# Column order of the split products in a hybrid decoder step: four interleaved sets of runs of 4 in place of two sets or one run

## The chip, the cores and the metric

The kernel runs on one core of a Trainium2 chip. The metric is the device time of one execution in microseconds, the median over repeated runs. A profiled execution, taken by the hardware profiler, gives the trace. TensorE does the matrix products, VectorE (DVE), ScalarE (ACT) and GpSimd (POOL) the element work, SyncE (SP) and others issue transfers. SBUF holds the operands, PSUM the results of TensorE, in banks of 512 fp32 columns on 128 partitions.

## The reference

One step of a one-layer decoder over 512 prompt rows and 64 sample rows (8 sequences of 8), everything in fp32, width 2048. The large products are the ones that matter here:

```python
h = rms_norm(x, g_mix) @ w_in            # 2048 -> 5128: q, k, v, forget gates, conv inputs
attn = fox_attention(q, k, v, logf)      # prompt: causal; sample: paged cache of 2048 rows
cy = conv_heads(u_ext, ...)              # gated, causal depthwise convolution, layer norm
x = x + concatenate([rms_norm(attn), cy]) @ w_out          # 2048 -> 2048
hid = square(relu(rms_norm(x, g_mlp) @ w_up))              # 2048 -> 8192
x = x + hid @ w_down                                       # 8192 -> 2048
gate = sigmoid(rms_norm(x, g_ple) @ w_ple_gate)            # 2048 -> 2048
y = rms_norm(x + (pe @ w_ple) * gate, g_final)             # pe: 256 -> 2048
```

## The kernel before

All activations lie transposed, features on the 128 partitions and the 576 rows (512 prompt, 64 sample) as columns. A product's moving operand and its result are 288 columns (`HR`), half of the rows, and both halves together make the 576. The weights, 128 x 128 blocks, are the stationary operand.

**Split products.** For precision every fp32 operand is split in two parts of the type fp32r: the rounded value ("hi") and the rest ("lo"). A product is then three matmuls into the same PSUM columns: hi x hi, hi x lo, lo x hi. ScalarE makes the hi parts (`split_hi`, line 160, and line 134 for the streamed weights), VectorE the lo parts (`split_lo`, line 163, and line 140).

**First phase** (to about 990 us). `mm6` (line 526) is the one place of its split products: three pairs of hi and lo, and in each pair the two halves of the columns, `r` = 0 and 1, into the two banks of one result `U`. The moving operands are `xh` and `xl`, the normed input; the weights `whi` and `wlo` come through `WStream`. It makes the input projection, the output projection and the projection of the per-layer input (there with the operands `px`). Between its products run the attention and the convolution: the cache pages (`k`, `v`) are read by lines 890 and 929, line by line paced by a credit per product. The forget gates' small projection (line 570) has 16 weight columns, reads the same `xh` and `xl`, and has no reordered columns.

**Second phase** (from about 990 us). `phase2` walks a list of weight blocks in the order of `plan`. For the up projection (`g` = 1) and the down projection (`g` = 2), each a 2 x 2 block product is made of seven products instead of eight: sums of weight blocks on one side (VectorE, lines 1913 to 1915) and of operand halves on the other, listed in `PRODS`. Each of the seven writes a bank `P` of its own; lines 1687 to 1689 are the three matmuls of one product. Line 1807 and its neighbours (`combine_head`, `combine_tail`) put the seven results together. The gate projection (`g` = 3, 4, 5) is made by `plain`, lines 1758 to 1760, in the ordinary way: the first block of outputs with both halves of the columns (`g` = 3), then the seven others for the first half of the columns (`g` = 4), then the same seven for the second half (`g` = 5), so that the end of the kernel has half the columns to finish.

**Order of columns.** `braid` (lines 91 and 92) changes the order in which a matmul walks its 288 columns, without moving any data. It sees the columns as (b a c): `c` neighbours form a run, `a` runs in a row belong to `a` different sets. It then goes through all runs of set 0, then all of set 1, and so on. Operand and result are walked in the same order, so every column still lands at its own place. Before, `a` is always 2. Line 526 uses `c` = 24: six runs of 24, then the other six. Lines 1687 to 1689 use `c` = 8: 18 runs of 8, then the other 18. `plain` uses `c` = 8 where both halves are in work (`g` = 3) and no reordering, one run of 288, where only one is (`g` = 4 and 5).

The order of the instructions on every engine is written out by the program (a manual schedule), with a queue of side work (`Beside`) that is charged by estimated costs; these costs do not depend on the order of columns.

Of the kernel before, what the change touches and what calls it, by code (L numbers as in the profile page):

```python
# [20 lines left out]
HR = 288  # L21
# [66 lines left out]
    return ap.bitcast(F32)  # L88


def braid(t, c):
    return t.rearrange("p (b a c) -> p a b c", a=2, c=c)


class Shift:
# [10 lines left out]
def EL(n):  # L106

    return n / 960.0 + 0.07
# [45 lines left out]
class Kern:  # L154
# [367 lines left out]
    def mm6(self, u, wh, wl, xh, xl, first, last):  # L522

        for n, (w, x) in enumerate(((wh, xh), (wh, xl), (wl, xh))):
            for r in range(2):
                self.nc.tensor.matmul(braid(u[:, r, :HR], 24), w, braid(x[:, r * HR:(r + 1) * HR], 24),  # L526
                                      start=first and n == 0, stop=last and n == 2)

    def chunk(self, u, c, k0, k1):
# [897 lines left out]
    def phase2(self):  # L1427
        tc, nc, a = self.tc, self.nc, self.a
# [36 lines left out]
        def rows_of(g):  # L1465
            return {3: (0, 1), 4: (0,), 5: (1,)}[g]
# [188 lines left out]
        for t, (si, k) in enumerate(quadlist):  # L1655
            g, p, *_ = segs[si]
            ks = self.orders[si]
            n, i = len(ks), t - seg0[si]
            if prev:
                pg, ppr, c, r, pfinal, pp_ = prev  # L1660
                if pg >= 3:
                    cost = self.plain_end(ppr, c, rb)
                else:
                    cost = self.combine_tail(ppr, EL)
                    c = c[0]
                bg.spend(cost)
                late = (pg, pp_) == (1, 31)
                fin_of[pg, pp_] = bg.add(2 if late else 0, fins[pg](pp_, c, r, pg if pg >= 3 else pfinal))
                if not late:
                    recent.append(fin_of[pg, pp_])  # L1670
                prev = None
            s = slots[min(g, 3), k]
            if s.work is not None:
                bg.flush(s.work)
                s = slots[min(g, 3), k]
            bg.spend(W.prep(t + 2))
            hi, lo = W.hl.pop(t)
            if i == 0:
                pr = {}
            if g >= 3:  # L1680
                self.plain(pr, hi, lo, s, i == 0, i == n - 1, rows_of(g))
            else:
                for (q, ia, ib) in self.PRODS:
                    if i == 0:
                        pr[q] = self.P_()
                    o, xh, xl = braid(pr[q][:, :HR], 8), braid(s.hi[:, ib, :], 8), braid(s.lo[:, ib, :], 8)
                    nc.tensor.matmul(o, hi[:, ia, :], xl, start=(i == 0), stop=False)  # L1687
                    nc.tensor.matmul(o, hi[:, ia, :], xh, start=False, stop=False)  # L1688
                    nc.tensor.matmul(o, lo[:, ia, :], xh, start=False, stop=(i == n - 1))  # L1689
            for fn in hooks.get(t, ()):  # L1690
                fn()
            if g == 2 and p in (4, 5, 6) and i in (0, 2):
                bg.nudge(2)
            slow = p == 0 and g != 2
            if i == (n - 2 if g < 4 else 5) and not slow:
                if g > 1:
                    bg.flush_all(0)
                r = pre[g](p, lastseg[g, p] == si)
            dt = (2.79, 3.18, 1.59, 1.59)[max(g - 2, 0)]
            if i == n - 1:  # L1700
                bg.wait(1000 + t, dt)
            else:
                bg.run(1000 + t, dt)
            if g == 1 and p == 0 and i + 2 < n and slots[1, ks[i + 2]].work:
                bg.flush(slots[1, ks[i + 2]].work)
            if i == n - 1:
                if g > 1:
                    bg.flush_all(0)
                if slow:
                    r = pre[g](p, lastseg[g, p] == si)  # L1710
                if recent[0]:
                    bg.flush(recent[0])
                if g >= 3:
                    c = t2.tile([128, 2, NR], F32, name="c", tag="c", bufs=3)
                else:
                    c = self.combine_head(pr, cx if (g, p) == (1, 31) else None)
                    bg.spend(2 * EL(HR))
                prev = (g, pr, c, r, lastseg[g, p] == si, p)
# [3 lines left out]
        pg, ppr, c, r, pfinal, p = prev  # L1722
        c, acc = c[:, :, :HR], self.acc2[:, HR:]
# [16 lines left out]
        o = next(rs)[:, None, :HR].broadcast_to([128, 2, HR])  # L1740
# [5 lines left out]
    def plain(self, pr, hi, lo, s, first, last, halves):  # L1746

        nc = self.nc
        for nh, blocks in enumerate(((2, 3), (0, 1))):
            for kh, ia in enumerate(blocks):  # L1750
                for r in halves:
                    if first and kh == 0:
                        pr[nh, r] = self.P_()
                    rows = slice(r * HR, r * HR + HR)
                    o, xh, xl = pr[nh, r][:, :HR], s.hi[:, kh, rows], s.lo[:, kh, rows]
                    if len(halves) == 2:
                        o, xh, xl = braid(o, 8), braid(xh, 8), braid(xl, 8)
                    nc.tensor.matmul(o, hi[:, ia, :], xh, start=first and kh == 0, stop=False)  # L1758
                    nc.tensor.matmul(o, hi[:, ia, :], xl, start=False, stop=False)  # L1759
                    nc.tensor.matmul(o, lo[:, ia, :], xh, start=False, stop=last and kh == 1)  # L1760
# [287 lines left out]
```

## Time and profile before

| | |
|---|---|
| median of 3 runs (lowest to highest) | 2654.57 us (2654.18 to 2655.11) |
| profiled execution | 2659.14 us |
| its span, first to last instruction | 2657.4 us |
| mean granted TensorE clock | 0.997 of full |
| busy share: TensorE, its weight loads, VectorE, ScalarE, GpSimd | 98%, 96%, 77%, 44%, 20% |
| TensorE instructions | 21,910 matmuls, 21,910 weight loads |
| moved by DMA | 543.87 MB, mean 205 GB/s |

How to read it. The profile's page lists groups of instructions: line, engine, operation, result<-operands, partitions x elements, the count, the busy time in us, the mean ns of one, and behind the bar the idle time before them with what ended it. A matmul is pipelined: its row lasts longer than the distance to the next one's start, so the mean ns of one is not what it costs in a stream. The distance from start to start is. The trace gives it by the window view (for a stretch of time: its length, and for each engine the busy time and the number of instructions, then granted clock, DMA share and GB/s; the order of the engines is TensorE's matmuls, its weight loads, VectorE, ScalarE, GpSimd), by the timeline (start in us, length in us, engine, line, operation, count), and by the chain of work that ended last in order of time (start, length, engine, result, line, count). All columns of a matmul are shown as one number (128x288) whatever their order.

### The profile page before, as it was taken

Reading aid. Unit: us, or ns where it says so; the run is one execution under the profiler, and the core shown is the slowest. Engines: PE = TensorE matmul, PEld = TensorE weight load, DVE = VectorE, ACT = ScalarE, POOL = GpSimd, SP = SyncE. Lnnn points to the kernel's source line nnn. Section 1 sums busy time; section 2 is a strip of 40 time slices with the busy share of each in tenths; the row PEclk is TensorE's granted clock in tenths of the full one; section 3 lists DMA queues with packets and bytes.
Section 4 is the critical chain, followed back from the end, with each engine's and each line's share of the span. In section 5 each row is a group of like instructions: output and inputs, shape, how many; then the busy total and the mean of one; then the engine's idle time right before and its main releaser. Section 6 shows DMA issues by size and latency. Waiting matters only on the chain.

```text
span 2657.4 us, 56481 instructions
## 1 busy us (share of the span) xinstructions
PE 2615.8 (98%) x21910; PEld 2539.0 (96%) x21910; DVE 2040.2 (77%) x3552; ACT 1166.7 (44%) x1714; POOL 527.4 (20%) x942
## 2 busy tenths in 40 slices
PE   9999999999999999999999999999999999999997
PEld 8999999888999999999999999999999999999997
DVE  6577778656564459889988888898888888898676
ACT  5222233245453335445554444554444444444554
POOL 2288787611020000000000000110000000000110
PEclk9999999999999999999999999999999999999998
DMA  6698998999764564444544444776575565656675
GB/s 206 207 309 289 309 294 293 301 322 325 239 222 128 183 212 144 152 143 160 171 158 143 142 143 142 256 197 196 153 205 145 165 174 169 176 188 216 199 244 166
DMA packets 240367, 543.87 MB, mean 205 GB/s; under 512 B 26049, under 2 KB 27074, under 8 KB 240098
## 3 DMA queue, kind: packets, MB, share of 16 engines
q1 hardware_dynamic: 170402, 325.97, 38.3%
q0 software_dynamic: 36160, 153.32, 18.2%
q10 hardware_dynamic: 33536, 60.96, 7.1%
q8 instruction: 172, 2.82, 0.4%
q14 instruction: 97, 0.79, 0.1%
HBM read 445.33 MB, written 94.83 MB: 203 GB/s over the span
## 4 chain that ended last, share of the span: by engine, by line
PE 87%; DVE 6%; DMA 4%; issue 2%; ACT 1%; SPq 0%; POOL 0%; ACTq 0%; DVEq 0%; POOLq 0%
PE U L526 24%; PE P L1687 16%; PE P L1689 16%; PE P L1688 16%; PE P L1759 2%; PE P L1760 2%; PE P L1758 2%; PE D L890 2%; PE O L929 2%; DVE w2l L163 1%; DMA wraw<-in_w_main 1%; DMA w2r<-in_w_down 1%; DMA k<-in_cache_kv 1%; DMA xs<-dl 1%; PE S L784 1%
## 5 line engine op out<-in xcount | busy, mean ns | idle before, releaser
L1687 PE MATMUL P<-xs,w2h 128*128 128x288 f32 x3584 | 1060.2, 296 | 12.1 <-DVE c L1807 7.2
L1688 PE MATMUL P<-xs,w2h 128*128 128x288 f32 x3584 | 1052.1, 294 | 0.0
L1689 PE MATMUL P<-xs,w2l 128*128 128x288 f32 x3584 | 1050.0, 293 | 0.5 <-DVE w2l L163 0.5
L160 ACT ACTIVATE w2h<-w2r 128x896 fp32r<-128x896 f32 (+1 forms) x632 | 558.9, 890 | 755.4 <-PE P L1688 420.8
L163 DVE TENSOR_TENSOR w2l<-w2r,w2h 128x896 fp32r<-128x896 f32 (+1 forms) x632 | 637.7, 1011 | 192.6 <-ACT w2h L160 190.3
L1687 PEld LDWEIGHTS P<-xs,w2h 128*128 128x128 f32 x3584 | 674.0, 188 | 19.5 <-DVE c L1807 10.3
L1689 PEld LDWEIGHTS P<-xs,w2l 128*128 128x128 f32 x3584 | 675.2, 188 | 1.5 <-DVE w2l L163 1.4
L1688 PEld LDWEIGHTS P<-xs,w2h 128*128 128x128 f32 x3584 | 673.6, 188 | 0.2 <-issue 0.2
L526 PE MATMUL U<-xh,whi 128*128 128x288 f32 x1792 | 397.2, 303 | 0.2 <-ACT xh L160 0.2
L526 PE MATMUL U<-xl,whi 128*128 128x288 f32 x1792 | 380.5, 293 | 0.8 <-DVE xl L354 0.7
L526 PE MATMUL U<-xh,wlo 128*128 128x288 f32 x1792 | 379.9, 293 | 0.1
L526 PEld LDWEIGHTS U<-xh,whi 128*128 128x128 f32 x1792 | 283.3, 188 | 18.9 <-issue 16.7
L134 ACT ACTIVATE whi<-wraw 128x512 fp32r<-128x512 f32 x224 | 140.8, 629 | 353.2 <-PE U L526 298.6
L526 PEld LDWEIGHTS U<-xl,whi 128*128 128x128 f32 x1792 | 284.8, 188 | 1.9 <-DVE xl L354 1.9
L526 PEld LDWEIGHTS U<-xh,wlo 128*128 128x128 f32 x1792 | 284.8, 188 | 0.3 <-DVE wlo L140 0.3
L140 DVE TENSOR_TENSOR wlo<-wraw,whi 128x512 fp32r<-128x512 f32 x224 | 160.2, 716 | 111.7 <-ACT whi L134 111.2
L1078 DVE SCALAR_TENSOR_TENSOR y<-ue,cv,y 128x512 f32<-128x512 f32 x240 | 183.5, 765 | 5.3
L1913 DVE TENSOR_TENSOR w2r<-w2r 128x512 f32<-128x512 f32 (+1 forms) x273 | 177.7, 651 | 11.8 <-DMA w2r<-in_w_down 11.8
L1079 POOL TENSOR_SCALAR cvt<-us,cv 128x64 f32<-128x64 f32 x240 | 161.2, 672 | 22.3
L1760 PE MATMUL P<-xs,w2l 128*128 128x288 f32 x512 | 150.9, 295 | 1.1 <-DVE w2l L163 1.0
L1759 PE MATMUL P<-xs,w2h 128*128 128x288 f32 x512 | 150.8, 295 | 0.8 <-DVE xs L1596 0.8
L1758 PE MATMUL P<-xs,w2h 128*128 128x288 f32 x512 | 151.2, 295 | 0.0
(413 smaller groups left out, 2791.1 us busy)
## 6 DMA issues: line engine op xcount, KB each, us to landing
k<-in_cache_kv SPq DMA_DIRECT2D x256, 256.0 KB, 4.4
v<-in_cache_kv SPq DMA_DIRECT2D x256, 256.0 KB, 4.5
w2r<-in_w_up SPq DMA_DIRECT2D x127, 512.0 KB, 3.9
w2r<-in_w_down SPq DMA_DIRECT2D x112, 512.0 KB, 3.8
wraw<-in_w_main ACTq DMA_DIRECT2D x156, 256.0 KB, 4.8
xs<-di POOLq DMA_DIRECT2D x32, 1008.0 KB, 7.3
w2r<-in_w_gate SPq DMA_DIRECT2D x60, 512.0 KB, 4.9
x<-c POOLq DMA_DIRECT2D x48, 576.0 KB, 5.8
```

The lines of the kernel that those rows point to most:

```text
L160: self.nc.scalar.activation(out, in_, AF.Copy, **kw)
L163: self.nc.vector.tensor_tensor(out, in_, f(hi), ALU.subtract)
L526: self.nc.tensor.matmul(braid(u[:, r, :HR], 24), w, braid(x[:, r * HR:(r + 1) * HR], 24), start=first and n == 0, stop=last and n == 2)
L1078: nc.vector.scalar_tensor_tensor(y, ue[:, j:j + NPR], w, y, ALU.mult, ALU.add)
L1079: nc.gpsimd.tensor_scalar(t, us[:, :, j:j + 8], w, None, ALU.mult)
L1687: nc.tensor.matmul(o, hi[:, ia, :], xl, start=(i == 0), stop=False)
L1688: nc.tensor.matmul(o, hi[:, ia, :], xh, start=False, stop=False)
L1689: nc.tensor.matmul(o, lo[:, ia, :], xh, start=False, stop=(i == n - 1))
L1758: nc.tensor.matmul(o, hi[:, ia, :], xh, start=first and kh == 0, stop=False)
L1759: nc.tensor.matmul(o, hi[:, ia, :], xl, start=False, stop=False)
L1760: nc.tensor.matmul(o, lo[:, ia, :], xh, start=False, stop=last and kh == 1)
L1913: lambda: V(w[:, :, 4:6, :], w[:, :, 0:1, :].broadcast_to([128, m, 2, 128]), w[:, :, 1:3, :], ALU.add),
```

## The change

All split products get the same order of columns: `a` = 4 and `c` = 4. The columns are seen as 18 groups of four runs of 4; a matmul walks the first run of each group (columns 0 to 3, 16 to 19, 32 to 35 and so on), then the second of each (4 to 7, 20 to 23 and so on), then the third, then the fourth. This holds for line 526, for lines 1687 to 1689, and for `plain` in all of `g` = 3, 4 and 5, where the condition goes. Nothing is added, removed or put in another place in any engine's order; behind the change the lines have numbers lower by one.

```diff
-def braid(t, c):
-    return t.rearrange("p (b a c) -> p a b c", a=2, c=c)
+def braid(t):
+    return t.rearrange("p (b a c) -> p a b c", a=4, c=4)
...
-                self.nc.tensor.matmul(braid(u[:, r, :HR], 24), w, braid(x[:, r * HR:(r + 1) * HR], 24),
+                self.nc.tensor.matmul(braid(u[:, r, :HR]), w, braid(x[:, r * HR:(r + 1) * HR]),
                                       start=first and n == 0, stop=last and n == 2)
...
-                    o, xh, xl = braid(pr[q][:, :HR], 8), braid(s.hi[:, ib, :], 8), braid(s.lo[:, ib, :], 8)
+                    o, xh, xl = braid(pr[q][:, :HR]), braid(s.hi[:, ib, :]), braid(s.lo[:, ib, :])
...
                     o, xh, xl = pr[nh, r][:, :HR], s.hi[:, kh, rows], s.lo[:, kh, rows]
-                    if len(halves) == 2:
-                        o, xh, xl = braid(o, 8), braid(xh, 8), braid(xl, 8)
+                    o, xh, xl = braid(o), braid(xh), braid(xl)
```

## The prediction

> **What bounds the kernel now.** I read the page first: the busy shares, the chain that ended last and the costliest groups.
>
> ```profile
> span 2657.4 us, 56481 instructions
> PE 2615.8 (98%) x21910; PEld 2539.0 (96%) x21910; DVE 2040.2 (77%) x3552; ACT 1166.7 (44%) x1714; POOL 527.4 (20%) x942
> PEclk9999999999999999999999999999999999999998
> PE 87%; DVE 6%; DMA 4%; issue 2%; ACT 1%; SPq 0%; POOL 0%; ACTq 0%; DVEq 0%; POOLq 0%
> L1687 PE MATMUL P<-xs,w2h 128*128 128x288 f32 x3584 | 1060.2, 296 | 12.1 <-DVE c L1807 7.2
> L1688 PE MATMUL P<-xs,w2h 128*128 128x288 f32 x3584 | 1052.1, 294 | 0.0
> L1689 PE MATMUL P<-xs,w2l 128*128 128x288 f32 x3584 | 1050.0, 293 | 0.5 <-DVE w2l L163 0.5
> L526 PE MATMUL U<-xh,whi 128*128 128x288 f32 x1792 | 397.2, 303 | 0.2 <-ACT xh L160 0.2
> L526 PE MATMUL U<-xl,whi 128*128 128x288 f32 x1792 | 380.5, 293 | 0.8 <-DVE xl L354 0.7
> L526 PE MATMUL U<-xh,wlo 128*128 128x288 f32 x1792 | 379.9, 293 | 0.1
> L1760 PE MATMUL P<-xs,w2l 128*128 128x288 f32 x512 | 150.9, 295 | 1.1 <-DVE w2l L163 1.0
> L1759 PE MATMUL P<-xs,w2h 128*128 128x288 f32 x512 | 150.8, 295 | 0.8 <-DVE xs L1596 0.8
> L1758 PE MATMUL P<-xs,w2h 128*128 128x288 f32 x512 | 151.2, 295 | 0.0
> ```
>
> TensorE has work in nearly every slice at its full granted clock, it makes 87% of the chain, and the big groups wait for next to nothing. So the time is the number of split products times the distance from one start to the next. The mean of 293 to 303 ns is not that distance: these matmuls overlap. Two more groups run line 526, in the listing of all TensorE forms:
>
> ```profile
> L526 PE MATMUL U<-px,wph 128*128 128x288 f32 x128 | 23.7, 306 | 0.7 <-ACT plt L1196 0.7
> L526 PE MATMUL U<-px,wpl 128*128 128x288 f32 x64 | 13.7, 295 | 0.0
> ```
>
> The counts are 3 x 1792 + 128 + 64 = 5568 at line 526, 3 x 3584 = 10,752 at 1687 to 1689, and 3 x 512 = 1536 at 1758 to 1760: 17,856 in all.
>
> Next I looked for the distance in stretches without a wait, since column order can act on nothing else. First line 526 (two sets, runs of 24), a row of the chain in order of time: start, length, count.
>
> ```profile
> 785.40 179.02 PE U L526 x1368
> ```
>
> That is 179.02 / 1368 = 130.86 ns. Then lines 1687 to 1689 (two sets, runs of 8) in three windows of 100 us, and lines 1758 to 1760 in the last stage, where one half of the rows is in work and the columns are contiguous: first half, then second half.
>
> ```profile
> 1200.00:1300.00 100.00, 100.00 (x762) 100.00 (x761) 89.95 (x140) 52.13 (x62) 10.26 (x19) 1.00 0.50 163
> 1300.00:1400.00 100.00, 100.00 (x762) 100.00 (x761) 91.83 (x145) 49.97 (x60) 8.64 (x16) 1.00 0.49 162
> 1400.00:1500.00 100.00, 100.00 (x762) 100.00 (x761) 87.27 (x136) 47.75 (x54) 8.08 (x15) 1.00 0.44 146
> 2480.00:2540.00 60.00, 60.00 (x458) 60.00 (x457) 39.20 (x67) 33.14 (x59) 7.09 (x10) 1.00 0.66 214
> 2570.00:2630.00 60.00, 60.00 (x452) 60.00 (x451) 43.79 (x75) 33.10 (x58) 13.14 (x20) 1.00 0.78 262
> ```
>
> A window also counts the matmuls begun up to 0.294 us before it (the mean of one), so runs of 8 give 100.294 us / 762 = 131.6 ns, three times alike; contiguous columns give 60.294 / 458 = 131.65 ns in the first half and 60.294 / 452 = 133.4 ns in the second, 132.5 on average. VectorE's and the DMA's load changes between these windows; the distance within one form does not. It belongs to the form and the operand's place.
>
> Two places hold operands and stage nearly fixed while the pattern differs. These timeline rows give the first matmul of a stretch and the first instruction behind it: 96 products of line 1758 to 1760 with both halves (two sets, runs of 8), then the 64 of line 570, which read the same xh and xl as line 526, but contiguously.
>
> ```profile
> 2430.67 0.29 PE L1758 MATMUL P<-xs,w2h 128*128 128x288 f32 x1
> 2443.26 0.95 PE L200 MATMUL P<-ones,acc 128*128 128x2 f32 x8
> 50.00 0.42 PE L570 MATMUL U<-xh,wfr 128*16 128x288 f32 x2
> 58.50 0.38 PE L691 MATMUL O<-cs,L 128*128 128x128 f32 x2
> ```
>
> 12.59 / 96 = 131.15 ns, against 132.5 contiguous; 8.50 / 64 = 132.8 ns contiguous, against 130.86 at line 526 (line 570 has 16 output rows, so that pair is less pure). So two sets take 1.35 to 1.95 ns off a product that is contiguous otherwise.
>
> **The change part by part.** No instruction is added, removed or moved on any engine; weights, counts, columns, accumulation groups and waits are the same. Only the order in which a product walks its 288 columns changes, in the operand and in the result alike: 72 runs of 4 where line 526 had 12 runs of 24, lines 1687 to 1689 36 runs of 8, and the one-half products a single run. No row shows four sets or runs of 4, so each term is bounded from both sides.
>
> *Sets.* One set to two gave -1.95 ns (line 570 to 526) and -1.35 ns (one half to both). I take half of such a step for two to four: -0.97 ns at line 526, -0.68 ns at the others. The ends are a whole further step and none.
>
> *Runs.* From 12 runs to 36 the distance rises by 131.6 - 130.86 = 0.74 ns, 0.031 ns a run, if the runs are what makes the difference. But those two stages also differ in their banks: line 526 alternates between two results, lines 1687 to 1689 write one three times running. The pair of the last stage, with 36 runs, is 0.45 ns quicker than lines 1687 to 1689 with as many, so most of the 0.74 lies elsewhere than in the runs. I take the runs at nothing; 0.031 ns each is the other end.
>
> [...]
>
> *Sum.*
> - Line 526: 5568 x -0.97 = -5.4 us (ends -10.9 and, by the runs, 60 x 0.031 x 5568 = +10.4).
> - Lines 1687 to 1689: 10,752 x -0.68 = -7.3 us (ends -14.5 and 36 x 0.031 x 10,752 = +12.0).
> - Lines 1758 to 1760: 192 with both halves, 192 x -0.68 = -0.1 us; 1344 contiguous, which also get the first step, 1344 x -2.03 = -2.7 us (ends -3.6 and about +0.3).
>
> Together -15.5 us. Does all of it reach the end? Two covers could take some away.
>
> ```profile
> 200.00:400.00 200.00, 200.00 (x2229) 183.20 (x2228) 151.46 (x262) 53.70 (x93) 159.06 (x289) 1.00 0.91 297
> PE P L1687 <- DVE c L1807: 7.2, 11, 1.0
> PE D L890 <- DMA k<-in_cache_kv: 3.2, 4, 1.2
> ```
>
> While the cache streams in, the DMA engines are 91% busy; 0.7% off TensorE's distances brings them to about 92%. VectorE is at 90% in the windows above and would come to 90.5%. The waits that would grow are those for the cache page and for VectorE's combination, 3.2 and 7.2 us in all today; half a per cent should add under 1 us, which I leave out. The profiled execution took 2659.14 us, 1.7 around its span and 4.6 over the median of 2654.57; it becomes 2643.6, and the median 2654.57 - 15.5 = 2639.1, forecast as 2639.
>
> **The rivals.**
> *Two sets were all there was.* Line 526 stands at 130.86 ns whichever half it reads, which looks like a floor. Then only the 1344 contiguous products gain, 1344 x -1.35 = -1.8 us: 2652.8, no change that can be told (0.2%, 5.3 us, is about what a measurement of this kernel resolves). Against: lines 1687 to 1689 stand above that floor. If these also came down to 130.86, another 10,752 x -0.74 = -8.0 us would bring 2644.8, still inside the forecast's side.
>
> *Runs of 4 are too short.* Every new run costs its 0.031 ns, in the reading of operands or the writing of results, and that outweighs what sets bring: +10.4 + 12.0 + 0.3 = +22.7 us, 2677; at half the price 2666. For it: distances rise from runs of 24 to runs of 8. Against: the one contiguous run is the slowest of all. It decides as soon as a run costs over about 0.02 ns, where the +15 us eat the forecast's gain. [...]
>
> [...]
>
> **How the numbers follow.** The forecast (a further step of between a third and two and a half times the one I took, -5.5 to -40 us) has 0.46; the closed gap 0.06; no change 0.20; runs too short 0.28, of which I give half to 2660 to 2672 and half to more. Faster 0.46 + 0.06 = 0.52, same 0.20, slower 0.28. The range leaves out the closed gap and the dearer half of the short runs, and reaches from 2605, where a step grows more than twice what I took and to which the forecast's tail thins out, to 2672. The forecast's own range is 2615 to 2649.
>
> **What would show it.** Right: in the windows 1200 to 1500 us over 766 matmuls each, the stretch of line 526 under 130 ns, and the last stage's two halves alike, both under 131.2. Wrong: 762 again with line 526 at 130.86 (two sets were all); distances that rise most at line 526, which gains most runs (runs too short); or a sum of starts that shrinks while waits for the cache pages or for VectorE's combination grow by as much. A count of matmuls or a granted clock that changes would make the whole argument void.

## The result and the profile after

| | before | changed |
|---|---|---|
| median (lowest to highest of 17 runs) | 2656.93 us (2652.48 to 2661.45) | 2650.78 us (2643.46 to 2654.84) |
| ratio of the times, 95% interval | | 0.9975 (0.9967 to 0.9984) |
| profiled execution, its span | 2659.14, 2657.4 us | 2648.39, 2646.6 us |

The change makes the kernel faster by a quarter of a per cent, 6 us of the 15.5 forecast. (The kernel before stands 2.4 us higher here than in the three runs that the prediction had.) The first lines of the changed kernel's page:

```profile
span 2646.6 us, 56485 instructions
PE 2602.3 (98%) x21910; PEld 2524.0 (95%) x21910; DVE 2038.7 (77%) x3552; ACT 1166.5 (44%) x1714; POOL 526.9 (20%) x942
PE 81%; DVE 7%; issue 5%; DMA 5%; ACT 1%; POOL 0%; SPq 0%; ACTq 0%; DVEq 0%; POOLq 0%
L1687 PE MATMUL P<-xs,w2h 128*128 128x288 f32 x3584 | 1052.4, 294 | 13.7 <-DVE c L1806 8.7
L526 PE MATMUL U<-xh,whi 128*128 128x288 f32 x1792 | 396.4, 302 | 0.0
```

Counts are the same and TensorE still sets the time (98% busy, 81% of the chain). Now the distances from start to start. First the stretch of line 526 in the output projection, in the chain in order of time; then a stretch of lines 1687 to 1689, and the two halves of the last stage, in the window view (TensorE's matmuls stand in the first bracket).

```profile
783.51 179.68 PE U L526 x1368
```

```profile
1400.00:1500.00 100.00, 100.00 (x767) 100.00 (x767) 87.11 (x137) 47.72 (x54) 8.06 (x15) 1.00 0.46 151
2470.00:2530.00 60.00, 60.00 (x471) 60.00 (x471) 40.97 (x70) 34.13 (x59) 7.06 (x10) 1.00 0.69 224
2570.00:2625.00 55.00, 55.00 (x419) 54.93 (x418) 37.04 (x63) 30.91 (x54) 7.96 (x12) 1.00 0.69 236
```

Line 526 takes 179.68 / 1368 = 131.35 ns where it took 130.86: it became slower here. Lines 1687 to 1689 take 100.29 / 767 = 130.8 in place of 131.6; the first half of the last stage 60.29 / 471 = 128.0 in place of 131.65, the second 55.29 / 419 = 132.0 in place of 133.4 (a few late starts included; 131.67 without them). So three of four places gained, by different amounts, and one lost.

Between the two traces the starts give the whole. The first start at lines 1687 to 1689 comes at 989.37 us before and 988.23 after, 1.1 us earlier: in the first phase the output projection lost 0.7 us at line 526, and the earlier stretches, 130.7 ns on average in place of 131.0, gained somewhat more. From there to the first start of the last stage it is 1441.30 us before and 1434.87 after, 6.4 us less: with the mean distances without waits (131.63 and 130.80 ns) the distances make 10,752 x -0.83 = -8.9 us, and the gaps over 145 ns grew from 26.0 to 28.5 us beyond the normal distance. The last stage, to the end of the span, takes 226.70 us before and 223.54 after, 3.2 us less. Together that is the 10.7 us between the two spans. The profiled pair is further apart than the medians; the experiment "history" below shows one thing in which executions of the changed kernel can differ.

### The profile page after: what moved, and what is told of

It is laid out like the page before. It is cut to its first block, busy times and chain, and to the rows that moved or that the text cites. A ratio compares the mean times of both kernels' runs of the same rounds, so it can differ in the third digit from the quotient of the medians.

```text
span 2646.6 us, 56485 instructions
## 1 busy us (share of the span) xinstructions
PE 2602.3 (98%) x21910; PEld 2524.0 (95%) x21910; DVE 2038.7 (77%) x3552; ACT 1166.5 (44%) x1714; POOL 526.9 (20%) x942
## 4 chain that ended last, share of the span: by engine, by line
PE 81%; DVE 7%; issue 5%; DMA 5%; ACT 1%; POOL 0%; SPq 0%; ACTq 0%; DVEq 0%; POOLq 0%
PE U L526 23%; PE P L1687 15%; PE P L1689 14%; PE P L1688 14%; PE P L1759 2%; PE P L1757 2%; PE P L1758 2%; PE D L890 2%; DVE w2l L163 2%; PE O L929 2%; DMA xs<-di 1%; DMA k<-in_cache_kv 1%; DMA w2r<-in_w_down 1%; DVE xs L163 1%; DMA xraw<-in_x 1%
```

## The experiments

All distances in the tables are from the starts in the traces, in stretches without a wait. "Output projection" is line 526 there; "up and down" is lines 1687 to 1689; "last, first half" and "second half" are lines 1757 to 1759 with one half of the columns in work.

**Contiguous columns; four sets of 24; two sets of 4; four sets of 8.** These separate the number of sets from the length of the runs. The theories: S, the number of sets sets the distance (mine); R, the length of the runs does; P, each order settles at each operand place in a distance of its own.

```diff
 def braid(t):
-    return t.rearrange("p (b a c) -> p a b c", a=4, c=4)
+    return t                                                # contiguous
+    return t.rearrange("p (b a c) -> p a b c", a=4, c=24)   # four sets of 24
+    return t.rearrange("p (b a c) -> p a b c", a=2, c=4)    # two sets of 4
+    return t.rearrange("p (b a c) -> p a b c", a=4, c=8)    # four sets of 8
```

> All split products with contiguous columns (no reordering at all). Theory S (the number of sets sets the distance): as line 570 and the old one-half products, 132 to 133 ns everywhere: line 526 at about 132.8 in the output projection (130.86 with two sets, 131.35 with four), lines 1687 to 1689 at about 132.5 (131.6 before, 130.7 after), the last stage at 131.65 and 133.4 as before; slower than the kernel before by 5568 x 1.9 + 10,752 x 0.9 = 20 us, 0.8%. Theory P (every order and operand place settles into a distance of its own, with no rule by sets or by run length alone): the last stage at 131.65 and 133.4, the others anywhere between 130 and 134.

> Four sets, but runs of 24 in place of 4. Theory S: as the changed kernel or lower, lines 1687 to 1689 at 130.7 or less, line 526 at 131.35 or less, the last stage near 127.9 and 131.7. Theory R (the run length sets it): line 526 at 130.83 as with two sets of runs of 24, lines 1687 to 1689 at about 130.9, the last stage near 131.0 in both halves. Theory P: distances of neither list, and not alike in the two halves of the last stage.

> Two sets, but runs of 4. Theory S: as before, lines 1687 to 1689 at 131.6, line 526 at 130.86, the last stage at about 131.1 in both halves; time within 0.2% of the kernel before. Theory R: as the changed kernel, lines 1687 to 1689 at 130.2 to 131.1, line 526 at 131.35 in the output projection, the last stage near 127.9 and 131.7; 0.25% faster. Theory P: neither list.

> Four sets of runs of 8. Theory S: as the changed kernel (127.9 and 131.7 in the last stage, 130.7 at lines 1687 to 1689). Theory R: as two sets of runs of 8, 131.6 at lines 1687 to 1689 and 131.1 in the last stage. Theory P: neither list.

| order | output projection | up and down | last, first half | last, second half | ratio to before, 95% |
|---|---|---|---|---|---|
| before (2x24, 2x8, 1 run) | 130.83 | 131.6 | 131.67 | 133.33 | 1 |
| changed (4x4) | 131.3 | 130.24 and 131.05 | 127.9 | 131.67 | 0.9975 (0.9967 to 0.9984) |
| contiguous | 133.3 | 131.75 | 131.67 | 133.33 | 1.0040 (1.0026 to 1.0055) |
| 4x24 | 133.33 | 132.4, later 133.65 | 133.33 | 133.33 | 1.0061 (1.0044 to 1.0078) |
| 2x4 | 131.1 | 132.4 | 132.2 | 133.33 | 1.0030 (1.0020 to 1.0039) |
| 4x8 | 133.3 | 132.5 | 132.8 | 132.9 | 1.0066 (1.0049 to 1.0082) |

A window each of the contiguous kernel, of the one with four sets of 24, of two sets of 4 and of four sets of 8:

```profile
1400.00:1500.00 100.00, 100.00 (x761) 100.00 (x760) 87.13 (x138) 46.91 (x55) 6.43 (x12) 1.00 0.41 137
```

```profile
1200.00:1400.00 200.00, 200.00 (x1513) 200.00 (x1512) 180.93 (x282) 101.41 (x120) 18.84 (x35) 1.00 0.49 162
1200.00:1400.00 200.00, 200.00 (x1513) 200.00 (x1512) 180.95 (x283) 101.61 (x120) 18.89 (x35) 1.00 0.49 162
1200.00:1400.00 200.00, 200.00 (x1512) 200.00 (x1511) 180.82 (x283) 101.61 (x120) 18.89 (x35) 1.00 0.49 162
```

Contiguous columns give 100.29 / 761 = 131.8 ns, four sets of 24 and two sets of 4 both give 200.29 / 1513 = 132.4, four sets of 8 give 200.29 / 1512 = 132.5. Four sets are slower than none at lines 1687 to 1689, with runs of 24 and of 8, and faster with runs of 4. Theory S falls. So does R: runs of 4 in two sets and in four sets are alike at line 526, but 1.7 to 4.3 ns apart at the other three places. And the first step, from one set to two, is hardly there at lines 1687 to 1689: contiguous columns stand at 131.75, two sets of 8 at 131.6. Line 526 had it, 133.3 to 130.83, and so had the last stage's first block: its 96 matmuls take 12.79 us with contiguous columns, 133.2 ns each, where two sets of 8 had 131.15. P stays.

**Forty-seven orders in one trace.** Another order in every outer block.

```diff
-                    o, xh, xl = braid(pr[q][:, :HR]), braid(s.hi[:, ib, :]), braid(s.lo[:, ib, :])
+                    m = MENU[si % len(MENU)]        # None, then 46 pairs (sets, run length)
+                    o, xh, xl = braid(pr[q][:, :HR], m), braid(s.hi[:, ib, :], m), braid(s.lo[:, ib, :], m)
```

> Another order of columns in every outer block, so that one trace shows the distances of 47 orders (contiguous and 46 pairs of sets and run length) at lines 1687 to 1689, and of some in the output projection and the last stage. The results are the reference's; the total time means nothing. Theory S: distances fall with the number of sets and do not care for the run length. Theory R: they go with the run length. Theory P: neither; distances between 128 and 135 ns scattered over the list, several orders below 130.2, which nothing in sets or run length foretells, and close to multiples of 0.83 ns.

Median distances in ns at lines 1687 to 1689; contiguous 131.75:

| run length | sets: distance |
|---|---|
| 2 | 2, 3, 4, 6, 8, 9, 12, 18, 24, 36: all from 247 to 325 |
| 4 | 2: 132.4, 3: 130.1, 4: 131.75, 6: 164.8, 8: 136.9, 9: 133.7, 12: 130.8, 18: 132.05, 24: 133.3, 36: 136.2 |
| 8 | 2: 131.6, 3: 136.5, 4: 132.5, 6: 128.9, 9: 134.0, 12: 131.75, 18: 137.1 |
| 12 | 2: 133.65, 3: 132.7, 4: 130.8, 6: 140.0, 8: 136.0, 12: 136.2 |
| 16 | 2: 134.6, 3: 133.3, 6: 134.6, 9: 135.6 |
| 24 | 2: 132.7, 3: 133.5, 4: 132.4, 6: 134.1 |
| 36, 48, 72 | 36 in 2: 131.75, in 4: 133.65; 48 in 2: 133.65, in 3: 132.4; 72 in 2: 133.65 |

Three blocks of that trace by the first and the last start of 126 matmuls (84 in the middle one): six sets of 8, three sets of 2, six sets of 4.

```profile
1965.89 0.29 PE L1702 MATMUL P<-xs,w2h 128*128 128x288 f32 x1
1982.13 0.29 PE L1702 MATMUL P<-xs,w2h 128*128 128x288 f32 x1
...
1288.07 0.44 PE L1701 MATMUL P<-xs,w2h 128*128 128x288 f32 x1
1309.62 0.44 PE L1701 MATMUL P<-xs,w2h 128*128 128x288 f32 x1
...
1736.40 0.34 PE L1703 MATMUL P<-xs,w2l 128*128 128x288 f32 x1
1757.16 0.34 PE L1703 MATMUL P<-xs,w2l 128*128 128x288 f32 x1
```

16.24 us / 126 = 128.9 ns, 21.55 / 84 = 256.5, 20.76 / 126 = 164.8. From runs of 4 up nothing goes with sets or run length: six sets are the best with runs of 8 (128.9 ns) and the worst with runs of 4 (164.8). Runs of 2 take about twice the time, 247 to 325 ns against 131.75 contiguous. Fewer orders than expected were under 130.2 (two), and many lay above the 135 expected. Nor do the distances keep to multiples of 0.83 ns, the step between the 130.83 and 131.67 of the runs ahead: 130.1, 131.75 and 132.4 are 156.2, 158.1 and 158.9 of them. The orders with runs of 4 came a second time later in the trace, in the same sequence, and gave the same distances within 0.4 ns. One entry stands out: 4x4 has 131.75 here and had 130.24 and 131.05 in the changed kernel, at the same place.

**One side alone.** The order on the operand or on the result alone, in the second phase.

```diff
+                    m, side = SIDES[si % len(SIDES)]
+                    mo, mx = m if side != "operand" else None, m if side != "result" else None
+                    o, xh, xl = braid(pr[q][:, :HR], mo), braid(s.hi[:, ib, :], mx), braid(s.lo[:, ib, :], mx)
```

> In the second phase the order is applied to both operand and result, to the operand alone, or to the result alone, in turn from block to block, for 4x4, 2x24, 2x8, 2x4 and 4x24 (sets x run length). With one side alone, the columns of the results are permuted; the amount of work is the same. If reading the operand from SBUF makes the difference (theory read), operand alone has the distance of both, and result alone that of contiguous columns, 131.75 ns. If writing to PSUM makes it (theory write), result alone has the distance of both, and operand alone 131.75.

| order | both | operand alone | result alone |
|---|---|---|---|
| 4x4 | 130.24 and 131.05 | 130.24 and 131.05 | 131.75 |
| 2x24 | 132.7 | 132.7 | 131.75 |
| 2x8 | 131.57 | 131.57 | 131.75 |
| 2x4 | 132.38 | 132.38 | 131.75 |
| 4x24 | 132.38 | 132.38 | 131.75 |

2x24 on both sides, on the operand and on the result, first and last of 84 matmuls each:

```profile
1429.62 0.30 PE L1697 MATMUL P<-xs,w2l 128*128 128x288 f32 x1
1440.77 0.30 PE L1697 MATMUL P<-xs,w2l 128*128 128x288 f32 x1
...
1451.91 0.30 PE L1697 MATMUL P<-xs,w2l 128*128 128x288 f32 x1
1463.06 0.30 PE L1697 MATMUL P<-xs,w2l 128*128 128x288 f32 x1
...
1474.31 0.29 PE L1695 MATMUL P<-xs,w2h 128*128 128x288 f32 x1
1485.37 0.29 PE L1695 MATMUL P<-xs,w2h 128*128 128x288 f32 x1
```

11.15 us / 84 = 132.7 twice, then 11.06 / 84 = 131.7. For five orders out of five the operand alone has the distance of both, and the result alone that of contiguous columns. (Late in the trace one block each of 4x4 on both sides and on the operand stood at 131.75, too; "history" comes back to this.) In these five, the whole effect is in reading the operand; how the result is written to PSUM makes no difference, 131.75 ns with runs of 4, 8 and 24 alike.

**Place of the operand, weight block, 16 weight columns.**

```diff
+                    m, kind, at = PLACES[si % len(PLACES)]
+                    ib, ia = at if kind == "x" else ib, at if kind == "w" else ia
                     o, xh, xl = braid(pr[q][:, :HR], m), braid(s.hi[:, ib, :], m), braid(s.lo[:, ib, :], m)
+                    if kind == "s" and 0 < i < n - 1:      # the three matmuls with hi[:, ia, :16], lo[:, ia, :16]
```

> In the up and down projection all seven products of a block read the same operand part (0 to 6), or the same weight block (0 to 6), or use 16 weight columns in place of 128 in the middle of the block, from block to block in turn, first with contiguous columns, then with 4x4. What is computed is not the reference's products, the amount of work is (but for the 16 columns). If the operand's place sets the distance (theory read), it differs between parts 0 to 6, with contiguous columns 131.67 at some and 133.33 at others as in the two halves of the last stage, and the weight block makes no difference, nor the 16 columns. If reading weights beside it sets it (theory weights), the distance differs between weight blocks, and with 16 columns it falls well below 130 ns.

4x4 reading operand part 0 alone, part 1 alone, and all parts with weight block 0, then with block 1; first and last of 105 matmuls each:

```profile
1341.42 0.29 PE L1700 MATMUL P<-xs,w2h 128*128 128x288 f32 x1
1355.09 0.29 PE L1700 MATMUL P<-xs,w2h 128*128 128x288 f32 x1
...
1363.31 0.29 PE L1702 MATMUL P<-xs,w2l 128*128 128x288 f32 x1
1377.19 0.29 PE L1702 MATMUL P<-xs,w2l 128*128 128x288 f32 x1
...
1495.67 0.29 PE L1700 MATMUL P<-xs,w2h 128*128 128x288 f32 x1
1509.39 0.29 PE L1700 MATMUL P<-xs,w2h 128*128 128x288 f32 x1
...
1517.62 0.29 PE L1700 MATMUL P<-xs,w2h 128*128 128x288 f32 x1
1531.34 0.29 PE L1700 MATMUL P<-xs,w2h 128*128 128x288 f32 x1
```

13.67 / 105 = 130.2 ns, 13.88 / 105 = 132.2, and 13.72 / 105 = 130.7 for both weight blocks. Over all parts, 4x4 gives 130.15 at parts 0, 2, 4 and 6 and 132.2 at parts 1, 3 and 5 (part 1 once 128.9); contiguous columns give 132.2 at the even parts and 131.1 or 132.2 at the odd ones. The parts lie 288 x 4 = 1152 bytes apart. The seven weight blocks agree in all but a few blocks, 131.75 contiguous and 130.24 and 131.05 with 4x4; 16 weight columns are 0.3 (contiguous) to 0.8 ns (4x4) quicker. So it is the operand's place, as theory read has it, though not with the distances that I had named (131.67 and 133.33), and not the weights beside it. What in their places tells odd parts from even ones is not shown; no spacing other than the 1152 bytes was run.

**Line 526 as before, the rest changed.**

```diff
-                self.nc.tensor.matmul(braid(u[:, r, :HR]), w, braid(x[:, r * HR:(r + 1) * HR]),
+                self.nc.tensor.matmul(braid2(u[:, r, :HR], 24), w, braid2(x[:, r * HR:(r + 1) * HR], 24),
```

> Four sets of runs of 4 at lines 1687 to 1689 and in the last stage as in the changed kernel, but line 526 with two sets of runs of 24 as before. If the changed kernel's gain comes from the second phase alone, as its distances say (line 526 130.86 before and 131.35 in the output projection after): the gain of the changed kernel stays, ratio 0.997 to 0.998, line 526 at 130.83 in the output projection. If line 526 had a share (its stretches before the output projection show 129.5 to 132): ratio 0.9985 or more.

Measured: ratio 0.9989 (0.9980 to 0.9998), 2652.89 us. By the ratio this is the second case, but its interval overlaps that of the changed kernel (0.9967 to 0.9984), and the trace does not bear it out: line 526 has its 130.83 again, and the first phase ends within 0.2 us of where it does in the changed kernel (988.35 and 988.23 us). What differs is lines 1687 to 1689, which are those of the changed kernel and did not keep their distance. Its window:

```profile
1200.00:1600.00 400.00, 400.00 (x3039) 400.00 (x3038) 355.15 (x555) 195.81 (x228) 33.32 (x62) 1.00 0.46 152
```

400.29 / 3039 = 131.7 ns, against 130.7 in the changed kernel for the same instructions on the same tiles. Behind a wait for a transfer at 1714 us it falls to 130.64, behind the next wait it is back at 131.75, and from about 1845 us on it stays at 130.64 for 500 us. So at one place one order has more than one distance.

**History.** The changed kernel with two foreign blocks: the ninth outer block in three sets of 4, the twenty-first contiguous.

```diff
+                    m = {8: (3, 4), 20: None}.get(si, (4, 4))
+                    o, xh, xl = braid(pr[q][:, :HR], m), braid(s.hi[:, ib, :], m), braid(s.lo[:, ib, :], m)
```

> The changed kernel, but the ninth outer block of the up projection uses three sets of runs of 4, and the twenty-first contiguous columns; all others keep 4x4. If an order has one distance of its own at a place: 130.24 and 131.05 in turn before, between and behind these two blocks. If the distance depends on what went before (4x4 behind 3x4 had 131.75 in the trace with 47 orders, and 130.24 and 131.05 behind contiguous columns in the trace with one side alone): 130.24 and 131.05 up to the ninth block, 131.75 between the two, 130.24 and 131.05 again behind the second.

Its windows ahead of the first, between the two, and behind the second foreign block:

```profile
1085.00:1170.00 85.00, 85.00 (x653) 85.00 (x652) 74.41 (x116) 40.11 (x46) 6.44 (x12) 1.00 0.45 148
1220.00:1440.00 220.00, 220.00 (x1671) 220.00 (x1671) 198.48 (x311) 109.25 (x128) 19.90 (x37) 1.00 0.48 159
1470.00:1590.00 120.00, 120.00 (x920) 120.00 (x920) 104.38 (x164) 56.38 (x65) 8.63 (x17) 1.00 0.45 149
```

85.29 / 653 = 130.6 ns, 220.29 / 1671 = 131.8, 120.29 / 920 = 130.75. Block by block it is 130.24 and 131.05 in turn, then 131.75 in all eleven blocks between, then 130.24 and 131.05 again, as expected of history. A wait does the same: behind one at 1710 us this trace drops back to 131.75, without any foreign block, and changes several times more behind later waits. So 4x4 does not have one distance here; it has two steady rhythms, 131.75 ns, and 130.24 and 131.05 in turn, and in these traces it changed from one to the other behind another order or a wait, at once or a few blocks later. Undisturbed it kept one for long: in the changed kernel's trace the better one held for 127 steps of 21 matmuls in a row, from 1357 us to the wait at 1706. Why a wait leads now to one and now to the other is open.

For 4x4 the better rhythm is worth 1.1 ns, 10,752 x 1.1 = 12 us over the second phase by estimate, if nothing else took it up. But something does. The changed kernel's profiled execution was in the better rhythm in 409 of its 511 steps of 21 matmuls; that of the kernel with line 526 as before was in 205, that of this kernel in 214. Their mean distances without waits differ by 0.45 ns, 4.8 us; the time from the first start at these lines to the last stage does not, 1434.9 us in the changed kernel, 1435.5 and 1434.8 in the other two. Their gaps over 145 ns were 24.2 and 23.6 us where the changed kernel's were 28.5. So in these three executions nearly all that the rhythm gives went into waits. In which rhythm the 17 timed executions ran is not recorded; that part of their spread of 11 us comes from there is not shown, and these three speak against much of it. The kernel before spread over 9 us too, though its one profiled execution kept 131.6 all through.

**Better orders.** Six sets of 8 everywhere, three sets of 4 everywhere, and six sets of 8 with three sets of 4 in the last stage's first half.

```diff
-    return t.rearrange("p (b a c) -> p a b c", a=4, c=4)
+    return t.rearrange("p (b a c) -> p a b c", a=6, c=8)    # or a=3, c=4
...
+                    m = (3, 4) if halves == (0,) else (6, 8)     # the third kernel, in plain
```

> The best of the 47 orders at lines 1687 to 1689, six sets of runs of 8, for all split products. Theory P with the operand's reading as the cause: the distances of that trace carry over, 128.9 ns at lines 1687 to 1689 (131.6 before), 128 to 129.4 at line 526 (130.86 before); together 10,752 x 2.7 + 5568 x 1.9 = 40 us off, ratio 0.985, the last stage unknown. If the distance depends more on history than on the order: between 128.9 and 132.3 at lines 1687 to 1689, ratio 0.99 to 1.0. If VectorE or the DMA become the bound first: the distances come as said and waits take their place.

> Three sets of runs of 4 for all split products. The distances of the trace with 47 orders carry over: 130.14 ns at lines 1687 to 1689, 130.0 at line 526; 10,752 x 1.46 + 5568 x 0.86 = 20 us off, ratio 0.9925. A theory by the number of sets gives something between two sets (1.003 with runs of 4) and four (0.9975).

> Six sets of runs of 8 everywhere but in the first half's part of the last stage, which takes three sets of runs of 4. There the distance falls from 133.33 ns (six of 8) to 126.67 (three of 4, as in the kernel with that order everywhere): 672 x 6.66 = 4.5 us less than the kernel with six of 8 alone, ratio 0.988. If the distance at that place depends on the order before it: between 126.7 and 133.3, ratio 0.988 to 0.99.

| order | output projection | up and down | last, first half | last, second half | median | ratio to before, 95% |
|---|---|---|---|---|---|---|
| 6x8 | 129.2 | 128.9 | 133.33 | 129.2 | 2630.32 us | 0.9896 (0.9883 to 0.9910) |
| 3x4 | 131.7 | 130.15 | 126.67 | 133.33 | 2645.56 us | 0.9958 (0.9946 to 0.9969) |
| 6x8, 3x4 in the first half | 129.2 | 128.9 | 126.67 | 129.25 | 2628.51 us | 0.9896 (0.9879 to 0.9912) |

Six sets of 8, a window and the waits of TensorE; then the first half of the last stage in the third kernel:

```profile
1400.00:1500.00 100.00, 100.00 (x778) 100.00 (x777) 88.60 (x139) 46.94 (x55) 6.44 (x12) 1.00 0.42 142
```

```profile
PE P L1687 <- DVE c L1806: 12.3, 16, 1.6
PE P L1687 <- DMA xs<-dl: 1.7, 1, 1.7
```

```profile
2455.00:2515.00 60.00, 60.00 (x476) 60.00 (x475) 40.65 (x69) 34.16 (x60) 7.09 (x10) 1.00 0.68 222
```

100.29 / 778 = 128.9 and 60.29 / 476 = 126.7, as forecast from the list. Six sets of 8 are 1% faster than the kernel before and beat the changed one too; it is not the 1.5% expected. The last stage's first half came at 133.33 in place of 131.67, 1.1 us lost, and part of the gain went into waits: that for VectorE's combination grew from 7.2 to 12.3 us, and all gaps over 145 ns at lines 1687 to 1689 from 26.0 to 37.0 us beyond the normal distance, against 29 us that the distances there brought. Here the covers that the prediction left out show plainly. Three sets of 4 missed their 0.9925 for two reasons: line 526 came at 131.7 in the output projection, not at 130.0, and the gaps at lines 1687 to 1689 grew from 26.0 to 32.6 us. The mixed kernel took its step of 6.7 ns in the first half; its time cannot be told from that of six sets of 8 alone.

## Why the prediction was right or wrong

- **The bound, right in the main.** Counts, clock and order of instructions stayed, and the row views showed the change place by place. But the time followed the distances only in part, as the covers below show.
- **Direction right; size wrong.** -15.5 us was forecast, -6 us came between the medians (-10.7 between the two traces). 2650.78 us lies outside the forecast's own range, 2615 to 2649, and inside the wider one to 2672 only because that one holds no change and slower outcomes as well.
- **The step that failed: sets.** "I take half of such a step for two to four" assumed that a further set always takes something off. It rested on two pairs. One compared line 570 with line 526: true at line 526 (133.3 contiguous, 130.83 in two sets), but not carried on, 4x4 came at 131.35 for a forecast 129.9. The other compared the last stage's first block with the blocks behind it, that is operands at other places, and its contiguous halves were themselves 1.7 ns apart: a sign of the place that I averaged away. At the block's own place the step was 2.1 ns (133.2 contiguous), not 1.35. At lines 1687 to 1689, with 60% of the products, contiguous columns stand only 0.15 ns over two sets, so there was no step to halve.
- **The terms**, in the two traces. Line 526: -5.4 us forecast, next to none measured (the output projection +0.7, the whole first phase -1.1). Lines 1687 to 1689: -7.3 forecast, -8.9 in the distances, -6.4 with the waits. The last stage: -2.8 forecast, -3.2 measured. The two that came near did so by accident, since the rule behind them is false.
- **Runs at nothing, right where it mattered.** 72 runs (three sets of 4) stood at 130.15, below the 36 runs of before. The rival's 0.031 ns a run is not there: two sets stand at 132.7 with 12 runs, 131.6 with 36 and 132.4 with 72. What is there is a step between runs of 4 and runs of 2 (247 ns and more, with operand and result both in runs of 2). Runs of 4 are not slow as such (130.1 ns in three sets, 130.8 in twelve), but six sets of them stand at 164.8 ns.
- **The floor, wrong.** "130.86 ns whichever half it reads, which looks like a floor": 128.9 ns (six sets of 8 at lines 1687 to 1689) and 126.67 ns (three sets of 4 in the last stage's first half) lie below it.
- **The closed gap, not shown.** The chances give it 0.06, with a time below the 2605 us where the range begins. No run shows the term; in its place the runs showed 126.67 ns as the lowest distance of a split product, and 2628.51 us as the lowest median.
- **The place, named but unused.** "It belongs to the form and the operand's place" was the right reading of the windows; the sum then used the form alone. And neither the prediction nor any rival saw that one order can have two distances.
- **The signs.** Of the three that were named for a right forecast one came about as said: 765, 763 and 767 matmuls in the three windows from 1200 to 1500 us, for 766. Line 526 did not go under 130 ns (131.35), and the last stage's halves were not alike (128.0 and 132.0).
- **Covers, mis-sized.** The prediction left out waits of under 1 us. In the changed kernel the gaps at lines 1687 to 1689 took back 2.5 of the 8.9 us; that alone shows little, since the two other traces with 4x4, at about 131.25 ns on average, had gaps of 24.2 and 23.6 us, less than the 26.0 at 131.63 before. Over the whole range, from four sets of 8 (132.57 ns on average, gaps of 20.0 us) to six sets of 8 (128.92 ns, 37.0 us), the distances give 39 us and the gaps take back 17. So by these two traces a gain in distance there is worth little more than half of itself, and this would have cut the forecast even with the right steps.

What stays open is the mechanism inside: why the starts stand further apart with one order of reading the operand than with another, and what the rhythms are made of.

## What to carry to other kernels

When matmuls of 4-byte operands stream without waits, measure the distance between starts for each order of the operand's columns at each operand place; a list of orders in one kernel, a block each, costs one run and here found 1%. Count the waits along with it: a part of what the distance gives can go there, here 17 of 39 us from four to six sets of 8. Do not draw a trend through two points of such a list, and do not average over operand places (130.15 and 132.2 ns with one order here). Before crediting a difference of 1 ns, look whether one execution holds the same distance throughout: here a wait or another order ahead switched 4x4 between 131.75 ns and 130.65 on average.

## What the runs showed of the hardware

- The order in which a result is written to PSUM did not change the distance in any of five orders with runs of 4 and more (131.75 ns); the order of reading from SBUF did (on the operand alone from 130.6 ns with 4x4 in its better rhythm to 132.7 with two sets of 24). With the order on both sides the distances at lines 1687 to 1689 go from 128.9 to 164.8 ns from runs of 4 up, and from 247 to 325 ns with runs of 2.
- The operand's place matters: 130.15 against 132.2 ns for even and odd parts with 4x4; the parts lie 1152 bytes apart.
- The steady rhythms are exact: blocks of 21 matmuls (pairs of them in 4x4's better rhythm) repeat to within 1 ns over hundreds of us: 2763 or 2764 ns in the kernel before, 2735 ns in turn with 2751 or 2752 in the changed one.
- 4x4 has at least two such rhythms at the same place, 131.75 ns, and 130.24 and 131.05 in turn. The changes between them came behind another order or a wait; the longest stretch in one, in the changed kernel's trace, was 127 such blocks.
